# A gated-linear-attention layer on one Trainium2 core: the decay's 16 inputs as columns of the value projection, in three passes

## The chip, the core and the metric

The kernel runs on one NeuronCore of a Trainium2 chip. Its engines are TensorE (PE in the profile; PEld are its weight loads), VectorE (DVE), ScalarE (ACT), GpSimd (POOL) and SyncE (SP), which here only issues transfers. Each works through a queue of its own in order; semaphores join them. The metric is the device time of one execution in microseconds (us).

## The reference, cut to what matters

A trunk of two layers for 256 tokens of width 1024. Each layer has a token mixer and a gated convolutional feed-forward network, each behind an RMSNorm that is scaled, shifted and gated by a modulation computed from a conditioning vector `c`. Layer 0 mixes by dilated attention; layer 1, where the change lies, by gated linear attention with 4 heads, keys of 128, values of 256 and chunks of 64 tokens:

```python
    mod = jax.nn.silu(c) @ w_ada[i] + b_ada[i]
    sh1, sc1, g1, sh2, sc2, g2 = [m[:, None, :] for m in jnp.split(mod, 6, axis=-1)]
...
    proj = h @ w_in          # q 512, k 512, v 1024, glr 16, r 1024 columns
    gk = jax.nn.log_sigmoid((glr @ w_gate + b_gate).astype(jnp.float32)) / B_TAU
...
    bcum = jnp.cumsum(gk, axis=3)
    q_t = q * jnp.exp(bcum)
    k_t = k * jnp.exp(-bcum)
    k_d = k * jnp.exp(blast - bcum)
    A = jnp.where(causal, jnp.einsum('bhncd,bhnsd->bhncs', q_t, k_t), 0.0)
    o_intra = jnp.einsum('bhncs,bhnse->bhnce', A, v)
    kv = jnp.einsum('bhncd,bhnce->bhnde', k_d, v)
...
    o = o_intra + jnp.einsum('bhncd,bhnde->bhnce', q_t, s_prev)
    o = rmsnorm(o, g_norm).reshape(B, S, B_V).astype(h.dtype)
    return (o * jax.nn.silu(r)) @ w_out
```

"The decay's inputs" are the 16 columns `glr`; the decay itself comes from `glr @ w_gate`.

## The kernel before, in words

All data are fp32. A product of two fp32 matrices is made of three fp32r matmuls (`mm3`, L199 to L201): each operand is split into a high part in fp32r and a low part, and high·high, high·low and low·high are added up in one PSUM bank. Weights are split in the kernel: `split` (L166 to L178) issues one load into a ring of four buffers (`raw`), copies each half to `whi` on ACT (L172) and subtracts on DVE for `wlo` (L178), from rings of three. A matmul has 128 rows of weights and up to 512 columns to stream. The activations `h` are kept transposed, eight tiles `h[kt]` of 128x256, high and low (`hhi`, `hlo`).

Layer 1's mixer goes in this order on PE:

- The norm and `early` (head 0's q for the input before its norm is known, L329).
- The values. The 1024 columns of `w_v_b` come in four loads of two k-tiles each. For each k-tile, two token tiles and two column halves of 512 are added up in four PSUM banks `pv`, so all 1024 columns are ready at the end.
- Between, `log_gates`: after four k-tiles, `glr` is made by 24 matmuls with 16 rows of weights padded to 128 and 256 tokens as columns, from a load `w_glr` of its own; DVE copies it (L1052). Then `gates_of` makes `z`, four fp32 matmuls of 16 rows (L1063, two records each), behind the values' sixth k-tile, and ACT and DVE turn these into the decays: `nz` (L1064), three passes for the log-sigmoid, `sp`, a scan `cs` (L1075), `dl` and the exponentials `e_d`, `e_q`, `e_k`, for head 0 and for heads 1 to 3 together.
- `states(hd)` for each head: the q/k projection `pqk` (48 matmuls of 256 columns; 24 for head 0) from a split of `w_qk_b`; DVE makes `k_d`, `q_t`, `k_t`; two fp32 transposes of `k_d` (L1141); scores `a` (L1152), chunk states `kv`. `products(hd)` makes the head's output `o` in fp32, `normed_output(hd)` its squares, their sum `oacc` on DVE, the rstd and the scaled output `on`. The heads' output stages lie behind the next head's projection.
- `gate(n)`: the projection `pr` for `r` (48 matmuls, a split of `w_r_b`), its silu, then `on * r`, split into `ohi` and `olo` (L1266, L1267). ACT changes its function table once (L1260) between the rstds and the silus.
- The output projection `py` (L199 to L201), which starts the tail to layer 1's feed-forward.

The modulation runs beside it: `next_ada` loads a chunk of `w_ada` (1 MB) into the `raw` ring (L133) and multiplies it on DVE with `c` (L140, two operations of 128x1024, the "dots"). Six chunks lie in this stage; their results are needed by the feed-forward's norm. In the kernel before, they are issued with the third and the fourth value load, three behind `gate(0)` and one behind `gate(1)`.

The order on each engine is fixed when the kernel is built: a scheduler places the instructions by modelled times, and `behind(...)` adds constraints by hand (an instruction may be put no earlier than those named). `bank(name, tag)` takes one of the eight PSUM banks (two of tag p, three of s, three of t).

Of the kernel before, what the change touches and what calls it, by code (L numbers as in the profile page):

```python
# [18 lines left out]
P = 128  # L19
D = 1024  # L20
T = 256
# [11 lines left out]
N_BUCKETS = 32  # L33
MAX_DISTANCE = 2048
# [23 lines left out]
def trunk(ctx: ExitStack, tc: tile.TileContext, I, out):  # L58
# [103 lines left out]
    def split(src, n, dmas=1, after=((), ()), late=(), low=(), lows=True):  # L162
# [5 lines left out]
        lo = wspl.tile([P, 2048], F32R, tag="wlo", name="wlo")  # L168
        for i in range(0, n, n // 2):
            c = slice(i, i + n // 2)  # L170
            with behind(*after[i > 0]):
                copied[0] = nc.scalar.copy(hi[:, c], raw[:, c])  # L172
        if not lows:
            return hi, lo, raw, n // 2
        for i in range(0, n, n // 2):
            c = slice(i, i + n // 2)
            with behind(*(late if i else low)):
                last_lo[0] = nc.vector.tensor_tensor(lo[:, c], raw[:, c], hi[:, c].bitcast(F32), op=ALU.subtract)  # L178
# [278 lines left out]
    def next_ada():  # L457
        if rest:
            ada_chunk(*rest.pop(0))
# [580 lines left out]
    w_g = gt([16, 512], "w_g")  # L1040
    nc.sync.dma_start(w_g, I["w_gate"])

    glr_copy = []

    def log_gates():
        with behind(*chain[5]):
            w_gl = split(I["w_glr"], 7 * 16 + P)
        ps = bank("glr", "t")
        for kt in range(KT):
            mm3(ps[:, :T], parts(w_gl, 16 * kt), h[kt], kt == 0, kt == KT - 1)  # L1050
        glr = gt([16, T], "glr")
        glr_copy.append(nc.vector.tensor_copy(glr, ps[:16, :T]))  # L1052
        return [gates_of(*part, glr) for part in PARTS]

    def gates_of(first, n, glr):
# [4 lines left out]
        for i in range(n):  # L1060
            hd = first + i
            ps = bank("z", "sttt"[hd])
            mm(ps[:, :T], w_g[:, P * hd : P * hd + P], glr, start=True, stop=True)  # L1063
            nc.scalar.activation(nz[:, T * i : T * i + T], ps[:, :T], AF.Identity,  # L1064
# [7 lines left out]
        nc.vector.scalar_tensor_tensor(sp, nz, 0.0, ea, op0=ALU.max, op1=ALU.add)  # L1072
# [6 lines left out]
        nc.vector.tensor_tensor(dl.rearrange("p (n c) -> p n c", c=CH), cs3,  # L1079
                                last.to_broadcast([P, 4 * n, CH]), op=ALU.subtract)  # L1080
# [33 lines left out]
    def states(hd):  # L1114
# [6 lines left out]
        else:  # L1121
            w = split(I["w_qk_b"][hd], 2048)
# [12 lines left out]
        nc.vector.tensor_tensor(k_t, pk, e_k[:, c], op=ALU.mult)  # L1135
# [243 lines left out]
```

## Time and profile before

| | |
|---|---|
| median of 3 runs | 765.38 us (763.9, 765.38, 782.7) |
| profiled execution | 764.38 us, span 762.6 us |
| busy: PE, DVE, ACT, POOL | 754.2, 649.4, 486.2, 33.6 us |
| DMA, mean rate over the span | 245 GB/s |
| layer 1's values, first matmul to first `pqk` | 463.34 to 490.58 us |
| first `py` matmul | 551.43 us |

The profile gives for each engine the time in which it executed something, the chain of work that ended last, groups of instructions by source line, and the records themselves. A record has a start, a length, engine, line, operation, output and inputs, and the shape of the output; "x4" means four alike in a row. Matmuls are pipelined, so the length of one is more than the time until the next can start; the cost of a matmul is read from start to start. An entry in square brackets is the idle time of the engine before the instruction and what ended it.

### The profile page before, as it was taken

Reading aid. Unit: us, or ns where it says so; the run is one execution under the profiler, and the core shown is the slowest. Engines: PE = TensorE matmul, PEld = TensorE weight load, DVE = VectorE, ACT = ScalarE, POOL = GpSimd, SP = SyncE. Lnnn points to the kernel's source line nnn. Section 1 sums busy time; section 2 is a strip of 40 time slices with the busy share of each in tenths; the row PEclk is TensorE's granted clock in tenths of the full one; section 3 lists DMA queues with packets and bytes.
Section 4 is the critical chain, followed back from the end, with each engine's and each line's share of the span. In section 5 each row is a group of like instructions: output and inputs, shape, how many; then the busy total and the mean of one; then the engine's idle time right before and its main releaser. Section 6 shows DMA issues by size and latency. Waiting matters only on the chain.

```text
span 762.6 us, 16024 instructions
## 1 busy us (share of the span) xinstructions
PE 754.2 (99%) x6394; PEld 731.5 (96%) x6394; DVE 649.4 (85%) x1185; ACT 486.2 (64%) x951; POOL 33.6 (4%) x56
## 2 busy tenths in 40 slices
PE   8999999999999999999999999999999999999997
PEld 6999999999999999999999998899999999999997
DVE  6997999898989678999999778797668999998592
ACT  6476676565566478776777456746766866666551
POOL 0001101101101010000000000000010000000100
PEclk9999999999999999999999999999999999999999
DMA  9988889778787357878556976875356777774631
GB/s 348 404 287 312 318 293 325 281 256 307 285 275 254 112 198 257 319 262 277 202 172 234 340 263 228 305 275 178 132 190 216 241 269 271 209 174 157 200 104 56
DMA packets 39225, 186.57 MB, mean 245 GB/s; under 512 B 9004, under 2 KB 11820, under 8 KB 25070
## 3 DMA queue, kind: packets, MB, share of 16 engines
q1 hardware_dynamic: 38768, 185.10, 69.6%
q8 instruction: 50, 0.82, 0.4%
q10 hardware_dynamic: 382, 0.45, 0.2%
q14 instruction: 25, 0.20, 0.1%
HBM read 184.43 MB, written 1.10 MB: 243 GB/s over the span
## 4 chain that ended last, share of the span: by engine, by line
PE 94%; DVE 3%; DMA 2%; issue 1%; ACT 0%; DVEq 0%; ACTq 0%
PE pab L199 10%; PE pab L200 10%; PE pab L201 10%; PE pqk L199 5%; PE pd L199 5%; PE pd L200 5%; PE pd L201 5%; PE pqk L201 5%; PE pqk L200 5%; PE pv L199 3%; PE pv L200 3%; PE pv L201 3%; PE pqk L675 2%; PE py L199 2%; PE py L201 2%; PE py L200 2%
## 5 line engine op out<-in xcount | busy, mean ns | idle before, releaser
L172 ACT CAST whi<-raw 128x1024 fp32r<-128x1024 f32 (+4 forms) x262 | 237.7, 951 | 92.6 <-PE pab L200 35.5
L178 DVE TENSOR_TENSOR wlo<-raw,whi 128x1024 fp32r<-128x1024 f32 (+3 forms) x246 | 263.8, 1097 | 38.5 <-ACT whi L172 37.5
L200 PE MATMUL pab<-hlo,whi 128*128 128x256 f32 x672 | 184.6, 276 | 0.0
L201 PE MATMUL pab<-hhi,wlo 128*128 128x256 f32 x672 | 184.6, 276 | 0.0
L199 PE MATMUL pab<-hhi,whi 128*128 128x256 f32 x672 | 183.2, 277 | 0.0
L200 PEld LDWEIGHTS pab<-hlo,whi 128*128 128x128 f32 x672 | 126.0, 188 | 0.2
L201 PEld LDWEIGHTS pab<-hhi,wlo 128*128 128x128 f32 x672 | 126.1, 188 | 0.0
L199 PEld LDWEIGHTS pab<-hhi,whi 128*128 128x128 f32 x672 | 125.1, 188 | 0.1
L140 DVE CUSTOM_DVE_ANT_0 ada_raw<-ada_raw,c_bc 128x1024 f32<-128x1024 f32 x96 | 114.1, 1229 | 4.7 <-DMA ada_raw<-in_w_ada 4.7
L199 PE MATMUL pqk<-hhi,whi 128*128 128x256 f32 x356 | 98.0, 281 | 0.0
L200 PE MATMUL pqk<-hlo,whi 128*128 128x256 f32 x356 | 97.4, 279 | 0.0
L201 PE MATMUL pqk<-hhi,wlo 128*128 128x256 f32 x356 | 96.8, 279 | 0.2 <-DVE wlo L178 0.2
L200 PE MATMUL pd<-glo,whi 128*128 128x256 f32 x308 | 84.8, 276 | 0.0
L201 PE MATMUL pd<-ghi,wlo 128*128 128x256 f32 x308 | 84.8, 276 | 0.0
L199 PE MATMUL pd<-ghi,whi 128*128 128x256 f32 x308 | 84.7, 276 | 0.0
L201 PEld LDWEIGHTS pqk<-hhi,wlo 128*128 128x128 f32 x356 | 65.9, 188 | 1.1 <-issue 0.7
L200 PEld LDWEIGHTS pqk<-hlo,whi 128*128 128x128 f32 x356 | 66.7, 188 | 0.1
L199 PEld LDWEIGHTS pqk<-hhi,whi 128*128 128x128 f32 x356 | 66.5, 188 | 0.1
L200 PEld LDWEIGHTS pd<-glo,whi 128*128 128x128 f32 x308 | 57.7, 188 | 0.0
L201 PEld LDWEIGHTS pd<-ghi,wlo 128*128 128x128 f32 x308 | 57.7, 188 | 0.0
L199 PEld LDWEIGHTS pd<-ghi,whi 128*128 128x128 f32 x308 | 57.7, 188 | 0.0
L962 ACT ACTIVATE r<-pab,small 128x256 f32<-128x256 f32 x86 | 47.5, 561 | 7.0 <-DVE r L965 6.7
(269 smaller groups left out, 1498.8 us busy)
## 6 DMA issues: line engine op xcount, KB each, us to landing
raw<-in_w_up SPq DMA_DIRECT2D x42, 1024.0 KB, 4.9
ada_raw<-in_w_ada SPq DMA_DIRECT2D x29, 1024.0 KB, 5.8
raw<-in_w_down SPq DMA_DIRECT2D x28, 704.0 KB, 4.3
ada_raw<-in_w_ada SPq DMA_DIRECT2D x38, 512.0 KB, 6.8
raw<-in_wqk SPq DMA_DIRECT2D x18, 1024.0 KB, 6.9
raw<-in_wv SPq DMA_DIRECT2D x14, 768.0 KB, 6.5
raw<-in_w SPq DMA_DIRECT2D x7, 960.0 KB, 6.5
raw<-in_w_out_a SPq DMA_DIRECT2D x4, 1024.0 KB, 6.9
```

Source lines behind the costliest of these rows:

```text
L140: i = nc.vector.tensor_tensor_reduce(w, w, c_bc, op0=ALU.mult, op1=ALU.add, scale=1.0, scalar=0.0, accum_out=dot,)
L172: copied[0] = nc.scalar.copy(hi[:, c], raw[:, c])
L178: last_lo[0] = nc.vector.tensor_tensor(lo[:, c], raw[:, c], hi[:, c].bitcast(F32), op=ALU.subtract)
L199: mm(ps, a[0], b[0], start=start, stop=False)
L200: mm(ps, a[0], b[1], start=False, stop=False)
L201: return mm(ps, a[1], b[0], start=False, stop=stop)
L675: mm(pqk[i], w[a], h[kt][b], start=s and i % 2 == 0 and (a, b) == (0, 0), stop=e and i % 2 == 1 and b == 1)
L962: nc.scalar.activation(r, u[:, :T], AF.Identity, scale=cw[2], bias=col(C_CB + 44 * l + f))
```

## The change

The value projection and the decay's inputs become one matrix of 1040 columns, the 16 inputs first, cut into three passes of 348, 346 and 346 columns (16+332, 346, 346). Each pass runs over all eight k-tiles and has two PSUM banks; its weights come in two loads of four k-tiles (768 KB each, 384 columns a k-tile with padding), of which only the real columns are split. Pass 0 therefore ends with `glr` for both token tiles in columns 0 to 15, tokens on the rows. `stack_parts` (DVE) writes its high part, its low part and the high part again beside each other at columns 0, 32 and 64 of `stacked`; `turn_parts` transposes both tiles on PE and copies them back. `w_gate` is laid out on the host three times below itself, at rows 0, 32 and 64, and rows 64 to 79 are replaced by its low part; so one fp32r matmul of 128 rows for each head gives all three products (`log_gates`).

The first halves of passes 0 and 1 run before the second half of pass 0. The values of a pass are copied out by one copy of ACT and one of DVE (`keep_values`). The constraint `offsets` places the second `sp` behind the first `dl`.

The six ada chunks are issued in other places: one with the second half of pass 1, one with the first half of pass 2, then with their dots behind head 1's `k_t`, behind `gate(0)`'s last low part, and behind `oacc` of heads 2 and 3. In the built order of DVE the last two pairs of dots stand directly behind the sums of squares of heads 2 and 3. Head 2's low parts stand behind head 0's `k_t`. `products(1)` is called inside `states(3)`, its second half behind head 3's transposes. In the built order of PE, the small matmuls of the mean square of heads 2 and 3 stand later within and behind `gate(1)`. Outside the stretch from the second last load before layer 1 to the output projection the order is the same on every engine.

```diff
+VCUTS = ((0, 332), (332, 346), (678, 346))
+STACKED = (0, 32, 64)
...
         mod[l, piece, kt] = m
         return i, j

-    def ada_chunk(l, n):
+    def ada_chunk(l, n, *after):
         raw = ada_load(l, n)
-        for s in range(2):
-            ada_dot(l, n, s, raw)
+        with behind(*after):
+            for s in range(2):
+                ada_dot(l, n, s, raw)


     last_load, copied, last_lo = [None], [None], [None]

-    def split(src, n, dmas=1, after=((), ()), late=(), low=(), lows=True):
+    def split(src, n, dmas=1, after=((), ()), late=(), low=(), lows=True, view=None):
         raw = wraw.tile([P, 2048], F32, tag="raw", name="raw")
         for i in range(dmas):
             c = slice(n * i // dmas, n * (i + 1) // dmas)
             last_load[0] = nc.sync.dma_start(raw[:, c], src[:, c])
         hi = wspl.tile([P, 2048], F32R, tag="whi", name="whi")
         lo = wspl.tile([P, 2048], F32R, tag="wlo", name="wlo")
+        part = view or (lambda w: w)
         for i in range(0, n, n // 2):
             c = slice(i, i + n // 2)
             with behind(*after[i > 0]):
-                copied[0] = nc.scalar.copy(hi[:, c], raw[:, c])
+                copied[0] = nc.scalar.copy(part(hi[:, c]), part(raw[:, c]))
         if not lows:
             return hi, lo, raw, n // 2
         for i in range(0, n, n // 2):
             c = slice(i, i + n // 2)
             with behind(*(late if i else low)):
-                last_lo[0] = nc.vector.tensor_tensor(lo[:, c], raw[:, c], hi[:, c].bitcast(F32), op=ALU.subtract)
+                last_lo[0] = nc.vector.tensor_tensor(part(lo[:, c]), part(raw[:, c]), part(hi[:, c].bitcast(F32)), op=ALU.subtract)
         return hi, lo

     def low_part(w, i):
...
-    def next_ada():
+    def next_ada(*after):
-            ada_chunk(*rest.pop(0))
+            ada_chunk(*rest.pop(0), *after)
...
+    def columns(n, half, **order):
+        c = (348, 346, 346)[n]
+        return split(I["w_v_b"][n, half], 4 * 384, view=lambda w: w.rearrange("p (k c) -> p k c", k=2)[:, :, 0:c], **order)
+
     with behind(*sixth):
-        w_first = split(I["w_v_b"][0], 2048, late=last_x[1:])
+        w_first = [columns(0, 0, late=last_x[:1]), columns(1, 0, low=last_x[1:], late=last_x[1:])]
     h, whole = all_normed(1, 0, "t", early)
     early_q = gt([P, T], "early_q")

     causal = gt([P, 2, P], "causal")
     nc.sync.dma_start(causal, I["causal"])
-    w_g = gt([16, 512], "w_g")
-    nc.sync.dma_start(w_g, I["w_gate"])
-
-    glr_copy = []
+    w_g = gt([P, 512], "w_g", F32R)
+    w_raw = gt([P, 512], "w_raw", tag="C1")
+    nc.sync.dma_start(w_raw, I["w_gate"])
+    with behind(*chain[7]):
+        nc.scalar.copy(w_g, w_raw)
+        own = slice(STACKED[2], STACKED[2] + 16)
+        nc.vector.tensor_tensor(w_g[own, :], w_raw[own, :], w_g[own, :].bitcast(F32), op=ALU.subtract)
+
+    stacked = gt([P, 2, P], "stacked", F32R)
+    nc.gpsimd.memset(stacked.bitcast(F32), 0.0)
+    glr = gt([P, T], "glr", F32R)
+    sums_of, low_rank, offsets = [], [], []
+
+    def stack_parts(pv):
+        for t in range(2):
+            hi, lo, again = (stacked[:, t, at : at + 16] for at in STACKED)
+            ps = pv[t][:, 0:16]
+            nc.vector.tensor_copy(hi, ps)
+            nc.vector.tensor_tensor(lo, ps, hi.bitcast(F32), op=ALU.subtract)
+            nc.vector.tensor_copy(again, hi.bitcast(F32))
+
+    def turn_parts():
+        ps = bank("glr", "t")
+        for t in range(2):
+            last = nc.tensor.transpose(ps[:, P * t : P * t + P], stacked[:, t, :].bitcast(F32), ident)
+        low_rank.append(nc.vector.tensor_copy(glr, ps[:, 0:T]))
+        return last

     def log_gates():
-        with behind(*chain[5]):
-            w_gl = split(I["w_glr"], 7 * 16 + P)
-        ps = bank("glr", "t")
-        for kt in range(KT):
-            mm3(ps[:, :T], parts(w_gl, 16 * kt), h[kt], kt == 0, kt == KT - 1)
-        glr = gt([16, T], "glr")
-        glr_copy.append(nc.vector.tensor_copy(glr, ps[:16, :T]))
-        return [gates_of(*part, glr) for part in PARTS]
-
-    def gates_of(first, n, glr):
+        for tg in "st":
+            ps = bank("z", tg)
+            for i in range(2):
+                hd = len(sums_of)
+                sums_of.append(ps[:, T * i : T * i + T])
+                last = mm(sums_of[hd], w_g[:, P * hd : P * hd + P], glr, start=True, stop=True)
+        return last
+
+    def gates_of(first, n):
         def new(name, tag, columns=n * T):
             return gt([P, columns], name, tag=f"{tag}{min(first, 1)}")

         nz = new("nz", "A")
         for i in range(n):
             hd = first + i
-            ps = bank("z", "sttt"[hd])
-            mm(ps[:, :T], w_g[:, P * hd : P * hd + P], glr, start=True, stop=True)
-            nc.scalar.activation(nz[:, T * i : T * i + T], ps[:, :T], AF.Identity,
+            nc.scalar.activation(nz[:, T * i : T * i + T], sums_of[hd], AF.Identity,
                                  scale=-1.0, bias=nbg[:, hd : hd + 1])

         ea = new("ea", "B")
...
-        nc.vector.scalar_tensor_tensor(sp, nz, 0.0, ea, op0=ALU.max, op1=ALU.add)
+        with behind(*offsets):
+            nc.vector.scalar_tensor_tensor(sp, nz, 0.0, ea, op0=ALU.max, op1=ALU.add)
-        nc.vector.tensor_tensor(dl.rearrange("p (n c) -> p n c", c=CH), cs3,
-                                last.to_broadcast([P, 4 * n, CH]), op=ALU.subtract)
+        offsets.append(nc.vector.tensor_tensor(dl.rearrange("p (n c) -> p n c", c=CH), cs3,
+                                               last.to_broadcast([P, 4 * n, CH]), op=ALU.subtract))
...

     pv = [[bank("pv", tg) for _ in range(2)] for tg in "ps"]
-    for n in range(4):
-        with behind(*((), chain[5], chain[7], glr_copy)[n]):
-            w = split(I["w_v_b"][n], 2048) if n else w_first
-            if n > 1:
-                next_ada()
-        if n == 0:
-            with behind(*chain[7]):
-                whole(early_q)
-        for i in range(2):
-            kt = 2 * n + i
-            for t in range(2):
-                ht = [y[:, P * t : P * t + P] for y in h[kt]]
-                for s in range(2):
-                    mm3(pv[t][s], ht, parts(w, D * i + 512 * s, 512), kt == 0, kt == KT - 1)
-        if n == 1:
-            gates = log_gates()
     v = [gt([P, D], f"v{t}") for t in range(2)]
-    for t in range(2):
-        nc.scalar.copy(v[t][:, 0:512], pv[t][0])
-        nc.vector.tensor_copy(v[t][:, 512:D], pv[t][1])
-
-    o_n = []
+
+    def values(n, half, w, kts=range(4), after=()):
+        c = (348, 346, 346)[n]
+        for j in kts:
+            kt = 4 * half + j
+            with behind(*after):
+                for t in range(2):
+                    ht = [y[:, P * t : P * t + P] for y in h[kt]]
+                    last = mm3(pv[n][t][:, 0:c], ht, parts(w, 384 * j, c), kt == 0, kt == KT - 1)
+        return last
+
+    def keep_values(n):
+        first, c = VCUTS[n]
+        at = 0 if n else 16
+        for t, copy in enumerate((nc.scalar.copy, nc.vector.tensor_copy)):
+            copy(v[t][:, first : first + c], pv[n][t][:, at : at + c])
+
+    values(0, 0, w_first[0])
+    last = values(1, 0, w_first[1])
+    with behind(*chain[3]):
+        w = columns(0, 1)
+    last = values(0, 1, w, after=[last])
+    with behind(*chain[7]):
+        whole(early_q)
+    stack_parts(pv[0])
+    with behind(*chain[7]):
+        w = columns(1, 1)
+        next_ada(last_lo[0])
+    last = values(1, 1, w, range(2), [last])
+    with behind(last):
+        last = turn_parts()
+    keep_values(0)
+    last = values(1, 1, w, range(2, 4), [last])
+    with behind(last):
+        last = log_gates()
+    pv.append([bank("pv", "t") for _ in range(2)])
+    gates = [gates_of(*part) for part in PARTS]
+    with behind(*low_rank):
+        w = columns(2, 0)
+        next_ada(last_lo[0])
+    keep_values(1)
+    last = values(2, 0, w, after=[last])
+    w = columns(2, 1)
+    values(2, 1, w, after=[last])
+    keep_values(2)
+
+    o_n, first_kt, accs = [], [], []
     last_a, last_sq, copies, kept = [None], [None], [None], [None, None]

-    def states(hd):
+    def states(hd, between=lambda turned: ()):
         if hd == 0:
             w = split(I["w_qk_b"][0][:, KT * P :], KT * P)
             pk = bank("pqk", "p")[:, :T]
...
-            w = split(I["w_qk_b"][hd], 2048)
+            w = split(I["w_qk_b"][hd], 2048, **(dict(low=first_kt[:1], late=first_kt[:1]) if hd == 2 else {}))
-        nc.vector.tensor_tensor(k_t, pk, e_k[:, c], op=ALU.mult)
+        first_kt.append(nc.vector.tensor_tensor(k_t, pk, e_k[:, c], op=ALU.mult))
-            nc.tensor.transpose(ps[:, c], k_d[:, c], ident)
+            last_kd = nc.tensor.transpose(ps[:, c], k_d[:, c], ident)
...
+        ahead = between(last_kd)
-            last = mm(d, kd[r, P * t : P * t + P], v[t][r, vh], start=True, stop=True)
+            with behind(*ahead):
+                last = mm(d, kd[r, P * t : P * t + P], v[t][r, vh], start=True, stop=True)
...
-    def products(hd, q_t, a_t, st):
+    def products(hd, q_t, a_t, st, last=None):
...
+            with behind(*([last] if last and et else [])):
...
+        accs.append(nc.vector.tensor_tensor(acc, sq[:, 0:T], sq[:, T : 2 * T], op=ALU.add))
...
     s1 = states(1)
     output(0, *s0)
     s2 = states(2)
-    po1 = products(1, *s1)
-    s3 = states(3)
-    normed_output(1, po1, last_a)
+    po1 = []
+
+    def ahead(turned):
+        po1.append(products(1, *s1, last=turned))
+        return last_o
+
+    s3 = states(3, ahead)
+    normed_output(1, po1[0], last_a)
     po2 = products(2, *s2)
     gate(0)
-    for _ in range(3):
-        next_ada()
+    low_0 = last_lo[0]
+    next_ada(first_kt[1])
     po3 = products(3, *s3)
     normed_output(2, po2, last_o)
     normed_output(3, po3)
             for s in range(2):
                 nc.scalar.copy(level[kt][s], h[kt][s])
     gate(1)
-    next_ada()
+    next_ada(low_0)
+    next_ada(accs[2])
     for n in range(4):

         if n > 1:
             gate(n)
+            if n == 2:
+                next_ada(accs[3])
         r = r_g[n]
         if n < 2:
             with behind(*norm_ops[1:]):
...
-    A["w_v_b"] = wb[:, 1024:2048].reshape(4, 2, P, D).transpose(0, 2, 1, 3).reshape(4, P, 2 * D)
-    A["w_glr"] = wb[:, 2048:2064].reshape(KT, P, 16).transpose(1, 0, 2).reshape(P, KT * 16)
-    A["w_glr"] = np.pad(A["w_glr"], ((0, 0), (0, P - 16)))
+    wv = np.zeros((KT, P, 3, 384), np.float32)
+    at = 0
+    for i, (first, n) in enumerate(VCUTS):
+        wv[:, :, i, 16 if i == 0 else 0 :][:, :, 0:n] = wb[:, 1024 + first : 1024 + first + n].reshape(KT, P, n)
+    wv[:, :, 0, 0:16] = wb[:, 2048:2064].reshape(KT, P, 16)
+    A["w_v_b"] = wv.reshape(2, 4, P, 3, 384).transpose(3, 0, 2, 1, 4).reshape(3, 2, P, 4 * 384)
-    A["w_gate"] = a["w_gate_b"][0]
+    A["w_gate"] = np.zeros((P, 512), np.float32)
+    for at in STACKED:
+        A["w_gate"][at : at + 16] = a["w_gate_b"][0]

```

More of the change, by code (lines that the diff above doesn't have):

```diff
@@ L1185, in products @@
             ev = slice(T * hd + P * et, T * hd + P * et + P)
-            for t in range(2):
-                d = po[:, T * et + P * t : T * et + P * t + P]
-                mm(d, v[t][:, ev], a_t[:, t, :], start=True, stop=False)
-                for n in range(2 * t, 2 * t + 2):
-                    if n:
-                        last_o[0] = mm(po[:, T * et + CH * n : T * et + CH * n + CH],
-                           st[n - 1][:, P * et : P * et + P], q_t[:, CH * n : CH * n + CH],
-                           start=False, stop=(n % 2 == 1))
+            with behind(*([last] if last and et else [])):
+                for t in range(2):
+                    d = po[:, T * et + P * t : T * et + P * t + P]
+                    mm(d, v[t][:, ev], a_t[:, t, :], start=True, stop=False)
+                    for n in range(2 * t, 2 * t + 2):
+                        if n:
+                            last_o[0] = mm(po[:, T * et + CH * n : T * et + CH * n + CH],
+                               st[n - 1][:, P * et : P * et + P], q_t[:, CH * n : CH * n + CH],
+                               start=False, stop=(n % 2 == 1))
         return po
```

1 line of the change is left out of this document (removed).

## The prediction

> **What bounds the kernel now.** I read the page's busy times, clock and chain first, then the busy times by window around the changed stretch, then TensorE's timeline there, and last the rows of VectorE (DVE), ScalarE (ACT) and the transfers that feed it. From the page:
>
> ```profile
> span 762.6 us, 16024 instructions
> PE 754.2 (99%) x6394; PEld 731.5 (96%) x6394; DVE 649.4 (85%) x1185; ACT 486.2 (64%) x951; POOL 33.6 (4%) x56
> PEclk9999999999999999999999999999999999999999
> PE 94%; DVE 3%; DMA 2%; issue 1%; ACT 0%; DVEq 0%; ACTq 0%
> ```
>
> TensorE is busy 99% of the span and is 94% of the chain that ended last. The windows' columns are length, then busy time (and instructions) of PE, PEld, DVE, ACT and POOL, then granted clock, DMA share and GB/s:
>
> ```profile
> 463.00:469.90 6.90, 6.90 (x32) 5.70 (x31) 6.90 (x14) 5.95 (x16) 0.00 (x0) 1.00 0.70 284
> 469.90:477.40 7.50, 7.50 (x45) 6.58 (x45) 6.16 (x12) 4.98 (x8) 0.00 (x0) 1.00 0.83 317
> 477.40:484.50 7.10, 7.10 (x32) 5.39 (x30) 6.17 (x9) 3.19 (x9) 0.00 (x0) 1.00 0.86 328
> 484.50:490.60 6.10, 6.10 (x28) 5.01 (x28) 3.89 (x5) 5.84 (x12) 0.00 (x0) 1.00 1.02 363
> 490.60:499.60 9.00, 9.00 (x78) 9.00 (x77) 8.91 (x14) 8.27 (x15) 0.00 (x0) 1.00 0.49 172
> 540.00:565.00 25.00, 25.00 (x222) 25.00 (x221) 18.48 (x32) 19.31 (x33) 1.12 (x2) 1.00 0.29 89
> ```
>
> PE fills each window at clock 1.00. So a us of TensorE work taken out here shortens the kernel by a us, as long as weights and splits keep up; and work added to DVE, ACT or the queues costs nothing until PE has to wait. DVE and ACT have holes up to 490 and nearly none from 490.6 to 499.6.
>
> **The change, part by part.** The sum is made against the profiled execution's 764.38 us (span 762.6 and 1.78 around it), 1.00 below the median 765.38 of the three runs. What TensorE does in the value stage (start, duration; a duration spans the pipeline, so cost is read from start to start):
>
> ```profile
> 463.34 0.59 PE L199 MATMUL pv<-whi,hhi 128*128 128x512 f32 x1
> 463.76 0.39 PE L200 MATMUL pv<-wlo,hhi 128*128 128x512 f32 x1
> ...
> 469.95 0.28 PE L199 MATMUL glr<-hhi,whi 128*128 128x256 f32 x1
> 470.19 0.40 PE L200 MATMUL pv<-wlo,hhi 128*128 128x512 f32 x1
> ...
> 474.85 0.28 PE L201 MATMUL glr<-hhi,wlo 128*128 128x256 f32 x1
> ...
> 477.44 1.09 PE L199 MATMUL pv<-whi,hhi 128*128 128x512 f32 x4
> ...
> 482.26 0.40 PE L199 MATMUL pv<-whi,hhi 128*128 128x512 f32 x1
> 482.59 1.99 PE L1063 MATMUL z<-glr,w_g 16*128 16x256 f32 x8
> 484.51 0.50 PE L200 MATMUL pv<-wlo,hhi 128*128 128x512 f32 x1
> 484.85 0.40 PE L201 MATMUL pv<-whi,hlo 128*128 128x512 f32 x1
> ...
> 490.58 0.28 PE L199 MATMUL pqk<-hhi,whi 128*128 128x256 f32 x1
> 490.70 0.28 PE L200 MATMUL pqk<-hlo,whi 128*128 128x256 f32 x1
> ```
>
> *Decay inputs' own products go.* 24 glr matmuls of 256 columns: two from 469.95 to 470.19 (0.24) and 22 from 474.85 to 477.44 (2.59): −2.83.
>
> *The gate sums.* Eight fp32 pass records from 482.59 to 484.51 take 1.92. The values' matmuls on either side take 0.33 (482.26 to 482.59) and 0.34 (484.51 to 484.85), where 0.23 is usual (next item), 0.21 for the turn to fp32 and back: −2.13. In their place stand four fp32r matmuls of 256 columns, with the three products stacked in 128 rows; by 490.58 to 490.70 each is 0.12: +0.47.
>
> *The values in three passes.* Of the 27.24 us from 463.34 to 490.58, 2.83 are glr, 1.92 z, 0.21 its turns, and 0.19 the first matmul's surplus (0.42 to the second start). The other 22.09 are 96 matmuls of 512 columns: 0.230 each, 0.449 ns a column. After, 144 matmuls of 348, 346 and 346 columns, 48 of each, make 49,920 columns for 49,152: +0.34. Does each of the 48 more cost something of its own? The rows nearest in width, of the first layer's values:
>
> ```profile
> 122.04 0.33 PE L199 MATMUL pv<-whi,hhi 128*128 128x384 f32 x1
> ...
> 122.56 0.34 PE L199 MATMUL pv<-whi,hhi 128*128 128x384 f32 x1
> ```
>
> 0.52 for three: 173 ns at 384 columns, 1 over 384 × 0.449. On the other side, 222 instructions of 256 columns in the window 540:565 take 25.00, 113 ns each, 2 under. So 0 to 5 ns each, allowing for rounding, 0 to 0.24; I take 0.12. The Trainium skill, "TensorE: Matmul & The Clock Gate", section "Back-to-back issue gap", speaks against the change: it gives a sustained 131 ns per matmul at 512 columns and 81 at 128, a large share of which does not shrink with the width. By it (an estimate on the line between the two) a 346-column matmul takes 109 ns, and 144 × 109 − 96 × 131 is +3.1 where my columns give +0.46; its sum would be −0.7, 763.6 us. The trace does not agree: 230 ns at 512, 173 at 384 and 113 at 256 lie nearly on a line through zero.
>
> *Two transposes* turn the stacked parts. The same pair in the heads:
>
> ```profile
> 505.88 0.38 PE L1141 MATMUL kdt<-ident,k_d 128*128 128x128 f32 x2
> 506.02 0.36 PE L199 MATMUL pqk<-hhi,whi 128*128 128x256 f32 x1
> 506.22 0.60 PE L1152 MATMUL a<-q_t,k_t 128*128 128x128 f32 x4
> ```
>
> 0.14 for the pair and 0.20 for the matmul behind it, 0.08 over 0.12: +0.22. *Head 1's products* now stand inside head 3's state work, cut by its transposes: one more turn between fp32 and fp32r, +0.21 by the z rows.
>
> PE's sum: −2.83 − 2.13 + 0.47 + 0.46 + 0.22 + 0.21 = **−3.60**.
>
> What is added elsewhere counts only where PE waits. VectorE:
>
> ```profile
> 68.00 0.16 DVE L543 TENSOR_SCALAR m<-m 128x2 f32<-128x2 f32 x1
> 473.71 2.35 DVE L178 TENSOR_TENSOR wlo<-raw,whi 128x1024 fp32r<-128x1024 f32 x2
> 477.64 0.41 DVE L1052 COPY glr<-glr 16x256 f32<-16x256 f32 x1 [1.59 <-PE glr L201]
> 482.54 1.27 DVE L178 TENSOR_TENSOR wlo<-raw,whi 128x512 fp32r<-128x512 f32 x2
> 486.54 2.36 DVE L178 TENSOR_TENSOR wlo<-raw,whi 128x1024 fp32r<-128x1024 f32 x2 [2.72 <-ACT whi L172]
> 498.38 1.22 DVE L140 CUSTOM_DVE_ANT_0 ada_raw<-ada_raw,c_bc 128x1024 f32<-128x1024 f32 x1
> ```
>
> *The stacking* is six DVE operations on 128x16. By L543 (0.16) and L1052 (0.41) they take 1.0 to 2.5; I take 1.2, nearest to the small row. Laid out from 463.34 with the costs above, pass 0 ends at 474.8; DVE, with one ada chunk's dots ahead of the stack (two of 1.15), is free at 475.6 and done at 476.8. PE has 12 matmuls of pass 1 between (1.9 us) and reaches the transposes at 476.7. The wait is 0 to 1.4; I take 0.1. The copy back (0.41, and one 128x332 of values ahead of it) is done near 477.9; z stands behind 12 more matmuls, at 479.0: nothing.
>
> *Splits.* Six loads of 768 KB, each split in two halves of 692 or 696 columns, take the place of four of 1024 KB and glr's 120 KB: ACT and DVE each do 8,320 columns for 8,432. The w_gate copy (128x512 on ACT, half of the 1.14 below) and its low part (16x512 on DVE, at most half of the 1.27 at 482.54) fall before 472, ahead of need at 479. The third pass's second half is the tight one: its low parts are done about 482.5 to 483, needed at 483.6. Cover: DVE's holes of 1.59 and 2.72 above, and ACT's here:
>
> ```profile
> 479.93 1.14 ACT L172 CAST whi<-raw 128x512 fp32r<-128x512 f32 x2 [2.88 <-DMA raw<-in_w_qk_b]
> ...
> 540.45 1.28 ACT L1260 ACT_TABLE_LOAD   x1
> ```
>
> *Head 2's low parts* are put behind head 0's k_t, which my layout has at 495.3; the first, 1.18 by 473.71, is done at 496.5, when PE reaches head 2: 0 to 0.3, and a us for each us that ACT or DVE slips before it; I take 0.1. Behind them on DVE stand the low parts of head 3, needed 5.6 us later (48 matmuls): time enough. Waits together +0.2, and the forecast is 764.38 − 3.60 + 0.2 = **761.0 us**.
>
> *The dots moved* (six ada chunks in this stage before and after, 2.3 us of DVE each) add no work. Two pairs now follow oacc of heads 2 and 3, ahead of the low parts of the gated outputs on DVE's queue. On SP's queue w_r3 waits behind an ada load that waits for w_r0's low part. The landing rows, and the start of the output projection:
>
> ```profile
> ada_raw<-in_w_ada SPq DMA_DIRECT2D x6, 1024.0 KB, 5.0
> raw<-in_w_r_b SPq DMA_DIRECT2D x4, 1024.0 KB, 6.1
> ```
>
> ```profile
> 510.48 5.40 SPq L166 DMA_DIRECT2D raw<-in_w_r_b  x2
> ```
>
> ```profile
> 551.43 0.28 PE L199 MATMUL py<-ohi,whi 128*128 128x256 f32 x1
> ```
>
> The row at 510.48 is two issues, so w_r3 left at 515.5; it now leaves near 525, when w_r1's low part frees its ada load, and by 6.1 lands 531, needed near 542: nothing. The output weights queued behind it left from 526 on and still do. The projection moves from 551.4 to about 548; in my layout the low parts of the outputs come 1.3 to 2 us before their matmuls. Head 1's products come earlier, at no cost beyond the turn.
>
> **The rivals.**
> *B, the low parts are late.* DVE is 8.91 of 9.00 busy in 490.6:499.6, so a slip there has no hole to vanish in. Against it: the change puts q/k work of head 2 exactly behind what frees it. The stack at its upper price (+1.3) and head 2 slipping by 1 us give 762 to 764; taken singly, 762.2 and 762.0.
> *C, slower: dots ahead of the gated outputs.* The two ada chunks behind oacc of heads 2 and 3 need loads that leave late. If one lands late, DVE stands with on and olo behind it, and py waits. For it: ACT's chain there is serial (ms, 540.45 table load, silu). Against: DMA share 0.29 in 540:565, a landing of 5.0. Up to 2 us late costs nothing; from 2 + 3.4 = 5.4 us late the kernel is slower than before; 7 to 9 us gives 766 to 768.
> *D, narrow matmuls bound by loading weights.* PEld, 188 ns a load in the row below; if each 346-column matmul took that instead of 157, 144 × 0.031 = +4.5: 765.5. Against it: those same loads stand before matmuls that start every 0.113.
>
> ```profile
> L200 PEld LDWEIGHTS pab<-hlo,whi 128*128 128x128 f32 x672 | 126.0, 188 | 0.2
> ```
>
> *E, nothing is gained:* the 3.4 us come back as a wait before the feed-forward, because its loads, not PE, set its start; 764.4. Against it: DMA share 0.29 there.
> *F, a fixed part in each matmul.* Were half of a 256-column matmul's 0.113 fixed and only the rest in proportion to columns, one of 347 would take 0.133 and one of 512 0.170: 144 × 0.133 − 96 × 0.170 = +2.8 for my +0.46, so 763.4. Against it: 512 columns take 0.230, not 0.170, twice the 256's time and more. The skill's rule above is of this kind.
>
> **How the numbers follow.** Forecast 0.63; B 0.18; C 0.07; D 0.03; E 0.06; F 0.03. The likeliest gives 761.0, its own range 759.5 to 762 (no waits and no cost per matmul 760.7, and 1 us for the spread of 763.9 to 765.38 among runs). Taking in B, F and E gives 759.5 to 764.8; C and D and some spread are left out. Two per cent, about what a measurement of this kernel can tell from no change, is 15.3 us: no case reaches it with a gain (PE's whole cut is 5), and only a mishap of several times C's price with a loss: faster 0.01, same 0.95, slower 0.04. The skill's page above, Part 1, says that an idle window of some 3.4 us halves the clock, which would add to a long wait; no window here shows a clock under 1.00.
>
> **What would show it.** Right: no glr matmuls; z about 0.5 us in four; pv's starts 0.157 apart; pqk of head 0 beginning about 487 (its first two inside pass 2); py starting near 548. Wrong: a PE wait ahead of the two transposes on stacked (stack too dear), at pass 2's second half or head 2's pqk released by wlo (B), at py released by olo with DVE waiting on ada_raw (C), or pv starts of 0.188 (D). The forecast fails if any one wait there is over 2 us.

## The result and the profile after

The changed kernel takes 761.15 us (median of 8 runs, 760.16 to 763.84) where the kernel before takes 764.97 (8 runs): a ratio of 0.9954, 95% interval 0.9941 to 0.9968. One run of the kernel before took 782.7 us, in a slower state of the chip, and the ratio leaves it out. The profiled execution took 760.93, span 759.1; the forecast was 761.0. The change is 0.46% and clear of noise: the interval is 0.14% to either side, much narrower than the two per cent that the prediction took for what can be told from no change.

The page of the changed kernel: span, busy times and the chain by engine, for the lines shown of before.

```profile
span 759.1 us, 16082 instructions
PE 750.4 (99%) x6416; PEld 732.7 (97%) x6416; DVE 650.8 (86%) x1195; ACT 485.7 (64%) x955; POOL 32.6 (4%) x57
PE 92%; DVE 4%; ACT 2%; issue 1%; DMA 0%; DVEq 0%; ACTq 0%
```

TensorE still bounds it: its busy time fell by 3.8 (754.2 to 750.4) and the span by 3.5. Its timeline in the value stage, for the rows of before (lines are four higher in the changed file):

```profile
462.99 0.51 PE L203 MATMUL pv<-whi,hhi 128*128 128x348 f32 x1
463.34 0.32 PE L204 MATMUL pv<-wlo,hhi 128*128 128x348 f32 x1
...
476.53 0.38 PE L1072 MATMUL glr<-ident,stacked 128*128 128x128 f32 x2
476.67 0.41 PE L203 MATMUL pv<-whi,hhi 128*128 128x346 f32 x1
476.91 0.32 PE L204 MATMUL pv<-wlo,hhi 128*128 128x346 f32 x1
...
478.64 0.64 PE L1082 MATMUL z<-glr,w_g 128*128 128x256 f32 x4
479.12 0.47 PE L203 MATMUL pv<-whi,hhi 128*128 128x346 f32 x2
...
483.27 0.28 PE L203 MATMUL pqk<-hhi,whi 128*128 128x256 f32 x1
483.39 0.28 PE L204 MATMUL pqk<-hlo,whi 128*128 128x256 f32 x1
483.51 0.33 PE L204 MATMUL pv<-wlo,hhi 128*128 128x346 f32 x1
...
486.96 0.29 PE L205 MATMUL pqk<-hhi,wlo 128*128 128x256 f32 x1
```

The 24 glr products are gone, z is 0.48 long (478.64 to 479.12) where it was 1.92, and the whole stage runs from 462.99 to 486.96: 23.97 for 27.24, and in it lie two matmuls of head 0 (0.24) that stood behind it before.

```profile
547.45 0.28 PE L203 MATMUL py<-ohi,whi 128*128 128x256 f32 x1
```

The table gives, for this kernel and all experiments, four stretches of TensorE's timeline: the values (first pv to the first matmul behind the last pv), the heads (on to the first pr), the gates (on to the first py) and the rest (on to the span's end), with the median of the timed runs and their ratio to the runs of before on the same chip.

| kernel | values | heads | gates | py to end | median | ratio (95%) |
|---|---|---|---|---|---|---|
| before | 27.24 | 35.75 | 25.10 | 211.2 | 764.97 | 1 |
| changed | 23.97 | 35.34 | 25.15 | 211.7 | 761.15 | 0.9954 (0.9941 to 0.9968) |
| e1 dots moved alone | 27.24 | 36.68 | 25.31 | 211.7 | 766.24 | 1.0026 (1.0014 to 1.0037) |
| e2 changed, dots as before | 23.96 | 36.30 | 25.11 | 211.7 | 762.64 | 0.9981 (0.9969 to 0.9992) |
| e3 stacked z alone | 25.59 | 42.99 | 25.32 | 213.7 | 772.02 | 1.0094 (1.0079 to 1.0109) |
| e4 changed, z in fp32 | 25.59 | 35.30 | 25.30 | 211.6 | 762.73 | 0.9982 (0.9972 to 0.9992) |
| e5 values in 256 columns | 27.34 | 35.56 | 25.11 | 211.1 | 765.14 | 1.0002 (0.9993 to 1.0010) |
| e6 changed, heads as before | 23.97 | 37.36 | 25.16 | 211.7 | 764.11 | 0.9986 (0.9975 to 0.9997) |
| e7 stack 2.8 later | 27.75 | 35.08 | 25.15 | 211.2 | 763.95 | 0.9989 (0.9981 to 0.9998) |
| e8 outputs 5 later | 23.97 | 35.19 | 25.30 | 211.8 | 762.32 | 0.9965 (0.9951 to 0.9979) |
| e9 stacked z, ordered | 25.60 | 36.37 | 25.31 | 212.0 | 764.22 | 1.0003 (0.9992 to 1.0014) |
| e10 stack 1.4 later | 24.77 | 35.17 | 25.15 | 211.9 | 762.03 | 0.9970 (0.9960 to 0.9980) |

The kernel before has a median of 764.87 on the chip of e1 to e4, 764.91 on that of e5 to e8 and 764.47 on that of e9 and e10. The ratio is worked out from the runs themselves and not from the two medians; a few runs of most kernels lie 2 to 4 us above the others, so ratio and medians can differ by 0.8 us (e2's medians make 0.9971). Each trace is one execution. So a difference of a us between two medians counts below only where the traces show where it lies.

### The profile page after: what moved, and what is told of

Same layout as the page of the kernel before. It is cut to its first block, busy times and chain, and to the rows that moved or that the text cites. A ratio compares the mean times of both kernels' runs of the same rounds, so it can differ in the third digit from the quotient of the medians.

```text
span 759.1 us, 16082 instructions
## 1 busy us (share of the span) xinstructions
PE 750.4 (99%) x6416; PEld 732.7 (97%) x6416; DVE 650.8 (86%) x1195; ACT 485.7 (64%) x955; POOL 32.6 (4%) x57
## 4 chain that ended last, share of the span: by engine, by line
PE 92%; DVE 4%; ACT 2%; issue 1%; DMA 0%; DVEq 0%; ACTq 0%
PE pab L203 10%; PE pab L204 10%; PE pab L205 10%; PE pqk L203 5%; PE pqk L205 5%; PE pd L203 5%; PE pd L204 5%; PE pd L205 5%; PE pqk L204 5%; PE pv L203 4%; PE pv L205 4%; PE pv L204 4%; PE py L203 2%; PE py L205 2%; PE py L204 2%; DVE ada_raw L142 2%
## 5 line engine op out<-in xcount | busy, mean ns | idle before, releaser
L182 DVE TENSOR_TENSOR wlo<-raw,whi 128x1024 fp32r<-128x1024 f32 (+5 forms) x248 | 263.8, 1090 | 31.0 <-ACT whi L176 30.2
L203 PE MATMUL pv<-whi,hhi 128*128 128x384 f32 (+2 forms) x160 | 53.2, 338 | 0.3 <-ACT v L628 0.3
```

Of the source, the lines that this page charges most:

```text
L182: last_lo[0] = nc.vector.tensor_tensor(part(lo[:, c]), part(raw[:, c]), part(hi[:, c].bitcast(F32)), op=ALU.subtract)
L203: mm(ps, a[0], b[0], start=start, stop=False)
```

## The experiments

Theory 1 is the prediction's: the gain is TensorE work taken out, and the moved dots and new orders only keep the other engines ahead of it. Its rivals: the moves bring a gain of their own, or each narrower matmul has a price beside its columns.

**e1: the kernel before with the dots moved.**

```diff
-    for _ in range(3):
-        next_ada()
+    low_0 = last_lo[0]
+    next_ada(first_kt[1])
...
-    next_ada()
+    next_ada(low_0)
+    next_ada(accs[2])
...
+            if n == 2:
+                next_ada(accs[3])
```

> The kernel before with one part of the change: the four ada chunks of the heads and gates get the places that the change gives them (dots behind head 1's k_t, gate 0's low part, oacc of heads 2 and 3). Theory 1 (the gain is TensorE work taken out; dots and orders are only cover): no TensorE work is changed, so 765.0, within 0.6. Rival 1 (the moved dots bring a part of the gain themselves, by freeing VectorE in the heads): 763.0 to 764.2. Rival 2 (the dots stand in the way of the gated outputs, and only the earlier finish pays for it): 766 or more.

It was slower by 1.4 (766.24 for 764.87 of the same chip). The values are unchanged; the heads are 0.93 longer and the gates 0.21. In the heads TensorE waits once, at head 3's kv. The wait (us in total, times, longest), then the rows around it:

```profile
PE kv L1164 <- ACT kdT L1143: 0.7, 1, 0.7
```

```profile
521.19 0.39 PE L1142 MATMUL kdt<-ident,k_d 128*128 128x128 f32 x2
521.39 0.60 ACT L1199 ACTIVATE osq<-o 128x512 f32<-128x512 f32 x1 [2.71 <-PE o L1192]
...
521.88 0.37 ACT L1143 COPY kdT<-kdt 128x256 f32<-128x256 f32 x1
...
522.30 0.48 PE L1164 MATMUL kv<-v,kdT 64*128 64x256 f32 x1 [0.72 <-ACT kdT L1143]
```

With the dots elsewhere the scheduler put head 3's kv directly behind its transposes, and the copy kdT between them, itself behind osq on ACT, lies open. (In the kernel before, the matmuls of an `o` stand between, from 519.76 to 522.13.) So the move alone costs; rival 1 falls, and theory 1's 765.0 is missed. Rival 2's value, 766 or more, fits, but not its cause: no py waits. No theory named an order that the scheduler changes on TensorE.

**e2: the changed kernel with these dots as before** (e1's edit undone in the changed kernel).

> The changed kernel with these four chunks back in the places of before (three behind gate 0, one behind gate 1). Theory 1: 761.2, within 0.6, and the matmuls from the values to the output projection as far apart as in the changed kernel (first pv to first py 84.5 us). Rival 1: 762.0 to 763.5. If the dots in the heads make low parts or k_t late, a wait shows on TensorE in the heads and costs its own length.

762.64, 1.5 over the changed kernel, of which the trace shows 1.0 in the heads again (36.30 for 35.34), by a wait of the same kind and length, here at head 2's kv:

```profile
PE kv L1220 <- ACT kdT L1197: 0.7, 1, 0.7
```

```profile
512.49 0.39 PE L1196 MATMUL kdt<-ident,k_d 128*128 128x128 f32 x2
...
513.61 0.48 PE L1220 MATMUL kv<-v,kdT 64*128 64x256 f32 x1 [0.72 <-ACT kdT L1197]
```

In the changed kernel ten pqk matmuls stand between these two, from 512.09 on, and nothing waits. So in the changed kernel the new places do keep about 1.0, and in the old one they lose as much. What pays is not where the dots stand by themselves but whether the TensorE order that goes with them covers kdT. Theory 1's 761.2 was missed for that; the values stand at 23.96 as it says.

**e3: the kernel before with the stacked gate sums alone.**

```diff
-        glr = gt([16, T], "glr")
-        glr_copy.append(nc.vector.tensor_copy(glr, ps[:16, :T]))
+        hi, lo, again = (stacked[at : at + 16, :] for at in (0, 32, 64))
+        nc.vector.tensor_copy(hi, ps[:16, :T])
+        nc.vector.tensor_copy(again, ps[:16, :T])
+        glr_copy.append(nc.vector.tensor_tensor(lo, ps[:16, :T], hi.bitcast(F32), op=ALU.subtract))
```

> The kernel before with the gate sums alone changed: glr keeps its own 24 matmuls, its high part, low part and high part again are written to rows 0, 32 and 64 of one tile, and z is four fp32r matmuls of 128 rows. Theory 1: the four fp32 sums and their two turns (2.13) go, four times 0.12 comes, so 1.66 less than before: 763.3; z is 0.48 long in the trace. If the copies, now three in a row on VectorE, hold z up, up to 1 us of it comes back: 764.3. If z was hidden anyway: 765.0.

The values became 1.65 shorter (25.59), as expected to 0.01. The kernel became 7 slower all the same. TensorE's longest wait, and the windows from it on, with the granted clock in the third column from the end:

```profile
PE kdt L1150 <- DVE k_d L1142: 4.6, 1, 4.6
```

```profile
497.00:502.00 5.00, 0.40 (x4) 0.20 (x3) 5.00 (x7) 3.04 (x6) 0.00 (x0) 0.86 0.83 308
502.00:505.00 3.00, 3.00 (x15) 2.96 (x16) 3.00 (x5) 0.94 (x4) 0.00 (x0) 0.50 0.82 270
505.00:508.00 3.00, 3.00 (x16) 2.62 (x15) 3.00 (x6) 1.23 (x2) 0.00 (x0) 0.59 0.68 178
508.00:512.00 4.00, 4.00 (x33) 3.74 (x32) 3.74 (x10) 1.04 (x4) 0.00 (x0) 1.00 0.95 358
```

Between the gate sums and head 0's k_d the scheduler now had put dots and low parts on VectorE:

```profile
495.18 1.21 DVE L140 CUSTOM_DVE_ANT_0 ada_raw<-ada_raw,c_bc 128x1024 f32<-128x1024 f32 x1
...
497.47 1.21 DVE L178 TENSOR_TENSOR wlo<-raw,whi 128x1024 fp32r<-128x1024 f32 x1
498.61 1.74 DVE L1084 TENSOR_TENSOR_SCAN cs<-keep,sp 128x768 f32<-128x768 f32 x1
500.27 1.19 DVE L178 TENSOR_TENSOR wlo<-raw,whi 128x1024 fp32r<-128x1024 f32 x1
501.39 0.41 DVE L1142 TENSOR_TENSOR k_d<-pqk,e_d 128x256 f32<-128x256 f32 x1
```

TensorE came 1.65 earlier to a k_d that came later (501.39, before 496.85), waited 4.6, and then ran at half clock for 5.6 us. The rest is 2.5 longer as well, near its end; there TensorE waits 1.4 for a sum of squares in the last feed-forward. Why that is late was not tried.

```profile
PE ms L871 <- DVE sqacc L226: 1.4, 1, 1.4
```

Theory 1 needed an amendment: the cut is worth its length only where VectorE's order keeps k_d ahead.

**e9: e3 with the change's orders** (e1's edit, the second sp behind the first dl, head 2's low parts behind head 0's k_t).

> The kernel before with the stacked gate sums of the run on z alone, and now also with the change's orders: the dots of four ada chunks in their new places, the second sp behind the first dl, head 2's low parts behind head 0's k_t. In the run on z alone, head 0's k_d stood behind two dots and low parts on VectorE and TensorE waited 4.8 for it. Theory 1, amended (TensorE's cut is worth its length where VectorE's order keeps k_d ahead; the orders are the cover): 763.3, at most 764.3 if kv of head 3 waits 0.9 for its kdT as in the run with the dots moved alone. Rival (k_d is late because the sums come too near to it, whatever the order): a wait of 2 or more at kdt stays, 766 or more.

```profile
PE pqk L202 <- DVE wlo L179: 0.2, 1, 0.2
```

The long wait is gone, and 764.22 is 7.8 under e3: these orders together are the cover; which of the three does it was not tried. Against the 764.47 of before on its chip it is only 0.25 less, not 1.66, and the ratio (0.9992 to 1.0014) does not tell it from no change. So theory 1's 763.3 is missed. In its trace the values keep their 1.64; heads and gates give back 0.83, of which two gaps of 0.35 and 0.21 over the usual spacing show, the first of them the wait above. Another 0.46 goes behind 577 to a slower pace that the last section describes. What else it lost is not settled.

**e4: the changed kernel with z in fp32.**

```diff
-    w_g = gt([P, 512], "w_g", F32R)
+    w_g = gt([16, 512], "w_g")
...
-            nc.vector.tensor_copy(hi, ps)
-            nc.vector.tensor_tensor(lo, ps, hi.bitcast(F32), op=ALU.subtract)
-            nc.vector.tensor_copy(again, hi.bitcast(F32))
+            nc.vector.tensor_copy(stacked[:, t, 0:16], pv[t][:, 0:16])
```

> The changed kernel with the decay's inputs still in the value columns, but z as four fp32 matmuls of 16 rows as before (no stacked parts, one copy and one transpose for each token tile). Theory 1: z 1.92 for 0.48 and two turns of 0.10: 1.65 more than the changed kernel, 762.8. With the run before this one the two parts add up: 24 glr matmuls for wider values are worth about 2.2 and the sums 1.65. If the parts are not independent (one wait that both remove), this run comes out near 761.2 or near 765.0.

762.73 for 762.8 expected; the values are 1.62 longer (25.59), and z is what it was before the change:

```profile
478.61 1.99 PE L1073 MATMUL z<-glr,w_g 16*128 16x256 f32 x8
```

So of the 3.8 between the medians 1.6 is the stacked sums, and the other 2.2 come with the decay's inputs in the value columns, with the orders in place for both. In the trace 1.9 of the 2.2 lie in the values (27.24 less 25.59, and the two pqk of 0.24).

**e5: the values' matmuls cut in two.**

```diff
-                    mm3(pv[t][s], ht, parts(w, D * i + 512 * s, 512), kt == 0, kt == KT - 1)
+                    for j in range(2):
+                        mm3(pv[t][s][:, T * j : T * j + T], ht, parts(w, D * i + 512 * s + T * j, T), kt == 0 and j == 0, kt == KT - 1 and j == 1)
```

> The kernel before with each 512-column matmul of the values cut into two of 256 columns: the same 49,152 columns in 192 matmuls for 96. It measures what a matmul costs beside its columns. Theory 1 with my forecast's 2.5 ns: +0.24, 765.2. The changed kernel's trace (144 matmuls of 347 columns at 158.6 ns against 230) says 8 to 9 ns: +0.8, 765.8. Rival F (half of a 256-column matmul fixed, 56 ns): the time per matmul of 256 stays 113 and that of 512 would have been 170, so the cut costs 5.4: 770. Rival D (bound by weight loads of 188 ns): +14, 779. By the Trainium skill, TensorE: Matmul & The Clock Gate, section Back-to-back issue gap (131 ns at 512 columns, 81 at 128, so 98 at 256, an estimate on the line between), the cut would cost 6.2.

765.14 for 764.91, and the values 27.34 for 27.24: 96 more matmuls cost 0.10, 1 ns each. That is a mean over two paces (last section): up to the glr products 256 columns start every 117.8 ns here, behind them every 113.3, while 512 start every 229 or 233 in the kernel before. At a like pace the cut costs between 2 ns less and 2 ns more for each 512 columns. Rivals D and F fall, and so does the reading of 8 to 9 ns that this run was to check. The Trainium skill's figures (TensorE: Matmul & The Clock Gate, Back-to-back issue gap) would make it 6.2, by the estimate above; the trace does not agree.

**e6: the changed kernel with the heads' orders as before** (no `low=first_kt` for head 2; `products(1)` ahead of `states(3)`).

> The changed kernel without the two orders in the heads: head 2's low parts are free to go where the scheduler puts them, and head 1's products are called ahead of head 3's projection as before. Theory 1: within 0.4 of 761.2, since TensorE's work is the same but for one turn of 0.1 to 0.2; the wait of 0.17 at head 2's first low part may go. Rival B (the order of the low parts is what keeps head 1 and head 2 fed): waits of 0.5 to 2 at a pqk released by k_t, kdt or wlo, 761.7 to 763.2.

764.11: 3.0 over the changed kernel. Theory 1's 761.2 is missed, and rival B's 763.2 is passed; the trace shows 2.0 of it, in the heads. Two waits, the first where head 2's low parts stand ahead of head 0's k_d, the second at head 3's kv as in e1:

```profile
PE kdt L1196 <- DVE k_d L1188: 1.9, 1, 1.9
PE kv L1220 <- ACT kdT L1197: 0.7, 1, 0.7
```

```profile
494.29 2.33 DVE L182 TENSOR_TENSOR wlo<-raw,whi 128x1024 fp32r<-128x1024 f32 x2
...
497.01 0.44 PE L1196 MATMUL kdt<-ident,k_d 128*128 128x128 f32 x2 [1.87 <-DVE k_d L1188]
```

In the changed kernel k_d and k_t go first (the row at 494.28 below).

**e7 and e10: the stack late.**

```diff
+    with behind(idle_work(4, last_dot[0])):
+        stack_parts(pv[0])
```

`idle_work(n)` puts n products of 128x512 on VectorE that nothing reads; e10 has 2.

> The changed kernel with four idle products of 128x512 on VectorE (about 0.59 each, 2.36) ahead of the stacked parts. It measures the cover of the stack. In the changed kernel's trace the stack ends at 475.98 and TensorE comes to the transposes at 476.53, a margin of 0.55, so the transposes should wait 1.8 and the time be 763.0; what follows on VectorE has more margin than that. If the transposes are hidden (the scheduler has other matmuls to put there): 761.2. If VectorE's queue has no slack behind it either, low parts of the third pass are late as well: 763.5 or more.

> The changed kernel with two idle products ahead of the stacked parts in place of four; one took 0.70, so 1.40. By the margin of 0.55 the transposes wait 0.85 and the granted clock stays 1.00: 762.0. With four (2.79, wait 2.2) the clock was 0.50 for the 3 us behind the wait, and the loss was larger than the wait. If the clock halves behind any wait at this place, this run loses 0.85 and about 1.6 more: 763.6.

An idle product took 0.70, not 0.59. With two, the transposes come 0.8 later (values 24.77 for 23.97) and the median is 762.03: 762.0 was expected. With four they come 2.2 later, as 2.79 less the margin of 0.55 says, but the stage grew by 3.78. Its windows:

```profile
476.00:479.00 3.00, 0.94 (x8) 0.68 (x7) 2.90 (x11) 1.53 (x3) 0.00 (x0) 1.00 0.67 249
479.00:482.00 3.00, 3.00 (x12) 3.00 (x11) 3.00 (x4) 0.70 (x2) 0.00 (x0) 0.50 0.02 3
482.00:486.00 4.00, 4.00 (x26) 4.00 (x26) 4.00 (x9) 3.69 (x11) 0.00 (x0) 0.95 0.94 354
```

Behind the wait the clock is 0.50 for 3 us, and a 346-column matmul starts every 0.29 (12 in the window) instead of 0.16: the other 1.6.

**e8: the gated outputs late** (`idle_work(4)` behind each of the last two pairs of dots; the scheduler spread them over the stretch from 528.8 to 551).

> The changed kernel with four idle products of 128x512 on VectorE behind each of the dots of heads 2 and 3 (4.7 in all between 529 and the output projection). It tests rival C of the prediction. Theory 1: VectorE has about 3 idle there, and the low parts of outputs and output weights come 1.9 to 2.4 ahead of their matmuls, so 4.7 costs 0 to 0.3: 761.2 to 761.5. Rival C (the dots behind oacc stand directly on the chain rstd, table load, silu, olo, py): 1.5 to 4.7 more, 762.7 to 765.9.

762.32, 1.2 over the changed kernel by the medians, but their intervals overlap (0.9951 to 0.9979 and 0.9941 to 0.9968). The trace, of the fastest of its six runs, shows 0.65: 0.5 at the first py matmuls, where the second follows the first by 0.30 for a usual 0.12, and 0.15 in the gates.

```profile
PEld py L205 <- DVE olo L1344: 0.2, 1, 0.2
```

That is more than theory 1's 0.3 and less than rival C's 1.5. Six of the eight products (0.69 each, 4.1 us) ran ahead of the first py and a seventh beside it. So this much added work uses up the margin of the outputs, and in the changed kernel no py waits for one.

## Why the prediction was right, step by step

- **glr's 24 matmuls, −2.83; z, −2.13 and +0.47.** Right: no glr product is left, e3 and e4 put z at 1.64 and 1.62 for my 1.66.
- **The values' columns, +0.46.** Too small. 23.97, less the two pqk (0.24), z (0.48), the transposes with the matmul behind (0.14 and 0.08) and the first matmul's surplus (0.19), leaves 22.84 for 144, 158.6 ns each. Before it was 22.09: +0.75. e5 shows that the number of matmuls is not the price (1 ns each); a 346-column one took between 157 and 160 from one stretch to the next, where 0.449 a column makes 155. What these 2 to 5 ns are stays open.
- **Transposes, +0.22.** Right: 0.14 and 0.24 for 0.16.
- **Head 1's turn, +0.21.** Not found as a loss: the heads with the two pqk added back (35.58) are 0.17 shorter than before. The pace of the last section, which I did not know, is as large as the difference: the 149 recorded pqk matmuls there that directly follow another start every 114.9 ns, before every 117.2, which makes 0.34.
- **The stack.** Priced at 1.2 with a wait of 0.1; the six operations take 0.61 and nothing waits. The margin of 0.55 was checked by e7 and e10.

```profile
475.37 0.25 DVE L1065 CAST stacked<-pv 128x16 fp32r<-128x16 f32 x2
475.57 0.17 DVE L1066 TENSOR_TENSOR stacked<-pv,stacked 128x16 fp32r<-128x16 f32 x1
...
475.89 0.49 DVE L1135 COPY v<-pv 128x332 f32<-128x332 f32 x1
...
494.28 0.41 DVE L1190 TENSOR_TENSOR k_t<-pqk,e_k 128x256 f32<-128x256 f32 x1
494.61 4.62 DVE L182 TENSOR_TENSOR wlo<-raw,whi 128x1024 fp32r<-128x1024 f32 x4
```

- **Head 2's low parts, 0 to 0.3, taken as 0.1.** 0.17: the first is done about 495.8, when TensorE has been ready for it since 495.7.

```profile
495.71 0.28 PE L204 MATMUL pqk<-hlo,whi 128*128 128x256 f32 x1
495.88 0.39 PE L205 MATMUL pqk<-hhi,wlo 128*128 128x256 f32 x1
496.10 0.29 PE L203 MATMUL pqk<-hhi,whi 128*128 128x256 f32 x1
```

  I treated this order as a risk. e6 shows that without it a wait of 1.9 stands in its place, which the rest of the change would have brought.
- **The moved dots, nothing.** The sum was right for the changed kernel, for a reason that I had not seen. By e1 and e2 the places of the dots decide a TensorE order worth about 1.0, either way. The prediction weighed the dots on VectorE's queue alone; the wait was at ACT's kdT.
- **py near 548.** 547.45; the prediction's rivals B, C, D, E and F did not come about.

The near hit has some luck in it. Against the profiled execution of before, the values came out 0.20 worse than forecast (−3.51 with the two pqk put back, for −3.71 with the stack's wait), the heads 0.48 better (−0.17 for +0.31); outside the stage the run started it 0.35 earlier and ended 0.5 later.

## What to carry to other kernels

On an engine that is busy throughout, read the gain from start to start of the instructions that go: that held to 0.04 where it was tested on z. Then ask of each one that is now early what it must still wait for: without the two orders in the heads (e6) only 0.8 of the 3.8 was left, and one part of the cut without any of the orders (e3) made the kernel 7 us slower. A part that adds no work can still move another engine's order, so look at the built order of every engine before you cost it at nothing.

## What the runs showed of the hardware

**Two paces.** The same 256-column matmul starts every 113.3 or every 117.8 ns, for tens of matmuls on end, at a granted clock of 1.00. Head 0's and head 1's projections in the kernel before, then in the changed one:

```profile
490.82 0.28 PE L201 MATMUL pqk<-hhi,wlo 128*128 128x256 f32 x1
...
494.00 0.28 PE L201 MATMUL pqk<-hhi,wlo 128*128 128x256 f32 x1
```

```profile
488.01 0.28 PE L205 MATMUL pqk<-hhi,wlo 128*128 128x256 f32 x1
...
490.73 0.28 PE L205 MATMUL pqk<-hhi,wlo 128*128 128x256 f32 x1
```

27 steps take 3.18 in the first (117.8) and 24 take 2.72 in the second (113.3). In the last feed-forward the changed kernel's run kept the slower pace for its first 13 us, some 100 matmuls. TensorE's windows of 25 us from 0.4 ahead of the first pab there, before and changed:

```profile
577.00:602.00 25.00, 25.00 (x218) 1.00 0.72 257
```

```profile
573.00:598.00 25.00, 25.00 (x213) 1.00 0.73 251
```

Five instructions fewer fit in, and 100 times 4.5 ns is 0.45 of the 0.5 by which the rest came out longer. In e5 the pace changes from 113.3 to 117.8 at 490.61, between the last pv and the first pqk, with neither a wait nor an fp32 matmul there. No run here sets it at will; what sets it stays open. Differences of half a us between two runs of this kernel need no other cause.

**Half clock behind a short wait.** In the profiled executions TensorE ran at half clock for 3.4 us behind e7's wait (2.1 idle, the transposes 2.2 late) and for 6.8 us from within e3's wait of 4.6; behind e6's wait of 1.9 and e10's 0.6 it did not. That is no threshold between 1.9 and 2.1. A half clock of 3.4 us lowers the mean granted clock of a run by 0.002; the runs without one lie at 0.998 to 1.000. Of the eleven timed runs of each, three of e7 (0.996) and three of e6 (0.996 or 0.997) lie below. So the same kernel meets it in some executions and not in others; where in the kernel a timed run meets it, its mean clock does not say.

In the traces the stretches at one clock between two changes are whole multiples of 3.413 us (467.63, 3.41 and 276.48 in e7; 491.52, 6.83 and 262.83 in e3). If the clock is set in such steps, what counts is how much of the wait falls into one step: e7's lies in one, e6's would be cut by a step into 1.2 and 0.7. This fits these traces and was not tried. The Trainium skill, TensorE: Matmul & The Clock Gate, Part 1, gives an idle window of about 3.4 us for the halving, and calls the window free-running; in e7 2.1 of idle time was enough. e7's median is 2.8 over the changed kernel, between the wait alone and wait and half clock together (3.8); but its four runs at a clock of 0.999 or more took 763.75 to 765.58, no less than the three at 0.996 (763.79 to 764.79), so the price of the half clock shows in the trace and not in the times.
